# Output projection, squared-ReLU MLP and final norm of an encoder layer: operands prescaled by the input row's norm, a pre-split first chunk, a last chunk by token halves

## The chip, the cores and the metric

One core of one Trainium2 chip runs the whole layer as one program. The metric is the time of one execution in microseconds (us), as the device measures it. Times below come from the runs of the kernel before and from one execution of it that the hardware profiler recorded.

## What is computed

The layer has three mixers on 1152 tokens (1024 of a prompt, 128 of running streams), a merge, an output projection, a channel mixer with a squared ReLU, and a final RMSNorm. D is 1024, the hidden width 4096, everything is float32. The change lies behind the mixers, save for one store and the order of two loads:

```python
def rms_norm(x, g):
    y = x * lax.rsqrt(jnp.mean(x * x, axis=-1, keepdims=True) + EPS)
    return y * g

m = sigmoid(g_a) * y_a + sigmoid(g_b) * y_b + sigmoid(g_c) * y_c
x = x + m @ w_o
u = rms_norm(x, g2) @ w_up
x = x + jnp.square(jax.nn.relu(u)) @ w_down
...
y = rms_norm(x, final_g)
```

## The kernel before

Activations lie transposed: channels on the 128 partitions, tokens along the free dimension, so that a token's norm is a sum over partitions and over 8 column tiles. Float32 accuracy is made from three products: each operand is split into a high part `h` (a cast on ScalarE to the rounded type fp32r) and a low part `l` (a subtraction, mostly on VectorE), and `mm3` multiplies h by h, h by l and l by h into one PSUM sum. Each matmul has 288 columns here (`HP`), two of them make a token half of 576 (`PC`).

Engines run their own instruction streams in order; the code's order is the order on each engine, and semaphores hold an instruction until its inputs are there. So the place of a line in the code decides what stands ahead of it on VectorE (DVE, `V`), ScalarE (ACT, `A`), GpSimd (POOL, `GP`) and on SyncE's DMA queue (SP, `SY`).

**Ahead of the change.** The y units (three mixers' output matrices) end with `y_finish`, which splits the merged m into `mh` and `ml` (L277, L278).

**Output projection (wo).** `back_half` runs 16 units: two token halves by 8 column tiles, 48 matmuls each (L230 to L232). `wo_load` fetches the weights, `wo_split` splits them (L1379, L1359). `Norm.take` adds the unit to the residual x on DVE (L1553), stores x to DRAM (`xs_d`, L1554), squares it on ACT (L1556), and POOL sums the squares.

**Second norm.** `Norm.stat` sums over partitions with small matmuls (L1565), takes the power -1/2 on POOL (L1568), makes a diagonal (L1570); `spread` broadcasts it by two matmuls and an ACT copy (L1581). Only then can `Norm.build` multiply x by norm and gain (L1587), form the Strassen combinations of a pair of column tiles (kk, kk+4) and split them into the operands `H` (ACT L1595, DVE L1359); `build3` splits the last ones. The first token half is built under the units of the second, the second half under the first up run.

**Up.** 16 steps, each a Winograd-Strassen 2 by 2 block: seven products (1, 2, 6, 5, 7, 4, 3) of 24 matmuls over both token halves; the first run is done once per token half (`ra`, `rc`). `SLOTS` fixes what happens between the products: a run issues its own 2, 6, 5, 7, then product 1 of the next run, then 4, 3. Products 1, 6, 7 and 4 add up in one PSUM tile Y, out of which ACT copies between them. `URun.after` makes the four blocks c11, c12, c22, c21, applies max(c,0)*c (`sq`, L1510; c21 on ACT, L1530 and L1531), forms s1 to s4 and stores seven operands (`put`, L1507) to `ad_d`.

**Down.** The 16 hidden steps are taken in `CHUNKS` of 3, 3, 3, 3, 2, 2; for each chunk four runs `d{chunk}{j}`, each seven products again, of 18 matmuls with three steps in the chunk and 12 with two. `feed` loads the operands back (`ar`, L1737) and splits them (ACT L1723, DVE L1359), at most two a slot. `Step.prep` splits the weights (ACT L1420, DVE L1359, four subtractions on POOL). `DRun.after` adds each product to `xt` (DVE, L1362), which `x_back` has loaded (L1710). PSUM has four tiles (`PD`), the pool `E` 16 tiles of 576 columns, the pool `T` 28 tiles of 1152.

**Tail.** After the last run `tail` squares x (ACT, sums on POOL and DVE, L1782, L1362), small matmuls sum over partitions (`fst`, L1815), then `fr` (L1817, L1818), `fdg` (L1821), `frb` (L1826), `frs` (L1828), and the last multiplications (DVE L1835, POOL L1832 and L1833) with the stores (L1837). It handles 576 columns at a time, hf 0 and then hf 1.

## Time and profile before

| | us |
|---|---|
| median of three runs (lowest, highest) | 2121.35 (2120.41, 2127.46) |
| the profiled execution | 2124.79 |
| its span, first to last instruction | 2123.0 |

| engine | busy us | share of the span |
|---|---|---|
| PE (matmul) | 2000.4 | 94% |
| DVE | 1423.1 | 67% |
| ACT | 806.9 | 38% |
| POOL | 798.8 | 38% |

The mean granted clock of TensorE is 0.977 of full speed. Stages, in time from the span's start: in-projection and mixers to 1038, y units to 1189, output projection to 1305, second norm and first up run to 1366, the other up runs to about 1690, six down chunks to 2088, tail to 2123. A PE that is busy is not a PE at its peak rate: what a stage loses is its length less the number of its matmuls times the time of one in an undisturbed stretch.

### The profile page before, as it was taken

The numbers are of one execution on the slowest core, as the hardware profiler recorded it, in microseconds if no ns is written. First come the engines' busy times: TensorE is split into PE (matmuls) and PEld (weight loads), VectorE is DVE, ScalarE is ACT, GpSimd is POOL, SyncE is SP. The second block draws the span as 40 slices with busy tenths as digits, with TensorE's granted clock in tenths as the row PEclk, the third lists the DMA queues.
The fourth block names the chain that finished last, engine by engine and source line by source line (L and its number), as shares of the span: only waits on it lengthen the run. The fifth ranks groups of instructions, "written<-read, shape, count | busy, mean of one in ns | idle before, by whom it ended". The sixth has DMA issues, their size and how long they took to land.

```text
span 2123.0 us, 37198 instructions
## 1 busy us (share of the span) xinstructions
PE 2000.4 (94%) x14321; PEld 1942.3 (91%) x14321; DVE 1423.1 (67%) x2243; ACT 806.9 (38%) x1501; POOL 798.8 (38%) x714
## 2 busy tenths in 40 slices
PE   8999999999999999999999997799999979999994
PEld 7999999999889999898999997699999979999893
DVE  6688888888755564756346456855565668767775
ACT  5434344343326454453212223332333434323431
POOL 4334533433622452626025224344444332222235
PEclk9999999999999999999999998899999989999997
DMA  5354553435544334332555252244343664424412
GB/s 177 121 144 136 128 148 102 113 106 135 171 139 146 132 100 138 119 122 82 201 193 177 89 167 88 82 145 151 132 148 134 215 231 146 157 93 138 132 56 89
DMA packets 202832, 287.66 MB, mean 135 GB/s; under 512 B 47032, under 2 KB 135928, under 8 KB 202656
## 3 DMA queue, kind: packets, MB, share of 16 engines
q1 hardware_dynamic: 202656, 285.29, 42.0%
q8 instruction: 113, 1.85, 0.4%
q14 instruction: 63, 0.52, 0.1%
HBM read 189.14 MB, written 96.08 MB: 134 GB/s over the span
## 4 chain that ended last, share of the span: by engine, by line
PE 51%; DVE 7%; POOL 5%; issue 4%; ACT 2%; DMA 2%; SPq 0%; DVEq 0%; POOLq 0%; ACTq 0%
PE u L230 6%; PE u L232 6%; PE u L231 5%; PE d L230 4%; PE d L232 4%; PE d L231 4%; PE pc L230 3%; PE pc L232 3%; PE pc L231 3%; PE y L232 2%; PE y L230 2%; PE y L231 2%; POOL g L1073 2%; POOL g L1074 1%; DVE a L1359 1%
## 5 line engine op out<-in xcount | busy, mean ns | idle before, releaser
L230 PE MATMUL pc<-hh,wh 128*128 128x384 f32 x1248 | 441.2, 354 | 7.5 <-ACT wh L201 5.2
L232 PE MATMUL pc<-hh,wl 128*128 128x384 f32 x1248 | 424.8, 340 | 2.0 <-DVE wl L213 2.0
L231 PE MATMUL pc<-hl,wh 128*128 128x384 f32 x1248 | 424.3, 340 | 1.1 <-DVE hl L377 1.0
L230 PEld LDWEIGHTS pc<-hh,wh 128*128 128x128 f32 x1248 | 237.0, 190 | 17.0 <-ACT wh L201 5.2
L231 PEld LDWEIGHTS pc<-hl,wh 128*128 128x128 f32 x1248 | 237.1, 190 | 4.6 <-DVE hl L377 3.1
L232 PEld LDWEIGHTS pc<-hh,wl 128*128 128x128 f32 x1248 | 236.4, 189 | 2.5 <-DVE wl L213 2.3
L1362 DVE TENSOR_TENSOR xt<-xt,d 128x576 f32<-128x576 f32 x168 | 126.1, 750 | 91.5 <-PE d L232 91.2
L539 DVE SCALAR_TENSOR_TENSOR y<-up,pv,y 128x768 f32<-128x768 f32 x120 | 132.1, 1101 | 0.2
L213 DVE TENSOR_TENSOR wl<-wr,wh 128x1024 fp32r<-128x1024 f32 (+1 forms) x71 | 92.5, 1305 | 55.6 <-ACT wh L212 55.5
L726 ACT ACTIVATE p<-s,m 128x128 f32<-128x128 f32 (+3 forms) x64 | 47.6, 744 | 178.2 <-DVE m L724 174.0
L542 POOL TENSOR_TENSOR y<-y,ud 128x256 f32<-128x256 f32 x120 | 107.8, 898 | 9.4
L1359 DVE TENSOR_TENSOR a<-ar,a 128x576 fp32r<-128x576 f32 x112 | 94.4, 878 | 13.5 <-ACT a L1723 13.3
L311 POOL TENSOR_TENSOR gt<-gt,gt 128x384 f32<-128x384 f32 x45 | 55.0, 1221 | 125.1 <-DVE gt L310 116.5
L541 POOL TENSOR_TENSOR ud<-up,pv 128x256 f32<-128x256 f32 x120 | 97.7, 814 | 7.4
L232 PE MATMUL y<-bh,wl 128*128 128x384 f32 x288 | 97.5, 339 | 0.0
L231 PE MATMUL y<-bl,wh 128*128 128x384 f32 x288 | 97.0, 337 | 0.0
L230 PE MATMUL y<-bh,wh 128*128 128x384 f32 x288 | 97.0, 337 | 0.0
L1723 ACT CAST a<-ar 128x576 fp32r<-128x576 f32 x112 | 72.5, 672 | 61.8 <-DMA ar<-ad_d 54.8
L230 PE MATMUL pt<-wh,hh 128*128 128x260 f32 (+1 forms) x288 | 84.9, 295 | 5.4 <-ACT vs L603 4.2
L212 ACT CAST wh<-wr 128x1024 fp32r<-128x1024 f32 (+1 forms) x71 | 74.1, 1046 | 38.2 <-PE y L231 29.0
L231 PE MATMUL pt<-wl,hh 128*128 128x260 f32 (+1 forms) x288 | 81.9, 284 | 0.9 <-DVE wl L213 0.9
L232 PE MATMUL pt<-wh,hl 128*128 128x260 f32 (+1 forms) x288 | 81.8, 284 | 0.0
(829 smaller groups left out, 6179.6 us busy)
## 6 DMA issues: line engine op xcount, KB each, us to landing
wr<-in_wu SPq DMA_DIRECT2D x67, 512.0 KB
ar<-ad_d SPq DMA_DIRECT2D x112, 288.0 KB
gt<-sg SPq DMA_DIRECT2D x24, 576.0 KB
wor<-in_wo SPq DMA_DIRECT2D x32, 256.0 KB
sg<-zgg_a SPq DMA_DIRECT2D x24, 192.0 KB
sg<-zgg_b SPq DMA_DIRECT2D x24, 192.0 KB
...
```

What stands on the lines that cost most here:

```text
L212: A.copy(h[:, :c], r[:, :c])
L213: V.tensor_tensor(out=l[:, :c], in0=r[:, :c], in1=h[:, :c].bitcast(F32), op=ALU.subtract)
L230: PE.matmul(out, lh, rh, start=start, stop=False, skip_group_check=again)
L231: PE.matmul(out, lh, rl, start=False, stop=False, skip_group_check=again)
L232: PE.matmul(out, ll, rh, start=False, stop=stop, skip_group_check=again)
L311: (V if n == 23 else GP).tensor_tensor(out=macc[ct][:, r], in0=macc[ct][:, r], in1=gt[:, r], op=ALU.add)
L539: V.scalar_tensor_tensor(out=y[:, :CD], in0=u[:, j:j + CD], scalar=w, in1=y[:, :CD], op0=ALU.mult, op1=ALU.add)
L541: GP.tensor_tensor(out=tm, in0=u[:, CD + j:NPR + j], in1=wp1, op=ALU.mult)
L542: GP.tensor_tensor(out=yp, in0=yp, in1=tm, op=ALU.add)
L1359: eng.tensor_tensor(out=out, in0=a, in1=b, op=ALU.subtract)
L1362: eng.tensor_tensor(out=out, in0=a, in1=b, op=ALU.add)
L1723: A.copy(t[:, 0:PC], r)
```

## The change

- **Norm factors.** The broadcast factors of the first norm (`rbs`), known since the start, are stored to DRAM (`rs_d`) and loaded as `s0` and `s1`. The up operands are built from x times gain times min(s, 1), and no longer wait for the second norm. The true norm comes in behind the up product, as a factor f in `sq`: DVE takes max(c,0)*f, ACT squares it. The matmuls in `fin` (24 instead of 12) and three small DVE instructions work out f.
- **Order in wo.** Column tiles go 0, 4, 1, 5, ... so that a pair is complete after two units; `build` and the splits stand inside the units from u = 2. Of the second half, build(3) and 16 splits are left for `ra`. m is held as `mm[pc][ct]`, h and l of one token half in a tile, so `y_finish` has pieces cut at token 576; `wo_load` and `wo_split(0)` stand one y unit earlier.
- **Up order.** Step 15 comes first, step 14 last.
- **First chunk split in up.** For steps 0 to 2, `put` splits the operand at once (ACT, DVE) and stores h and l to `ah_d`; chunk 0 loads 21 tiles of 1152 columns and splits nothing. `x_back(1..3)` go into d00, d01 and d02.
- **Down.** Chunks 3, 3, 2, 3, 3, 2. Every third operand split of `feed`, and the weight splits of products 5 and 7, are on POOL.
- **Last chunk.** Four runs by token halves: columns j = 0, 1 and 2, 3 of the first half, then 2, 3 and 0, 1 of the second, each matmul still 288 columns; the weights of two j stand in one step and are kept. `final(0)` normalises and stores the first token half under the last two runs; `final(1)` does the rest behind them, from PSUM, with three of eight columns on ACT and POOL.

The diff, cut to what the text speaks of, with twelve columns of indentation left out:

```diff
-CHUNKS = (3, 3, 3, 3, 2, 2)
+CHUNKS = (3, 3, 2, 3, 3, 2)
+CTS = (0, 4, 1, 5, 2, 6, 3, 7)
...
+        SY.dma_start(rs_d[:, r], rbs[g])
...
-        sub(V, l, self.raw(p), raw(h))
+        sub(GP if p in self.gp else V, l, self.raw(p), raw(h))
...
     def put(self, p, n):
-        SY.dma_start(v2(ad_d[p, self.s])[:, self.pcs[0]:self.pcs[-1] + 1, :], self.buf(n))
-
-    def sq(self, c):
-        V.scalar_tensor_tensor(out=c, in0=c, scalar=0.0, in1=c, op0=ALU.max, op1=ALU.mult)
+        b, c = self.buf(n), slice(self.pcs[0] * HP, (self.pcs[-1] + 1) * HP)
+        if self.s < CHUNKS[0]:
+            h, l = E(f"{self.name}h{p}"), E(f"{self.name}l{p}")
+            A.copy(v2(h).bitcast(F32R), b)
+            V.tensor_tensor(out=v2(l).bitcast(F32R), in0=b, in1=v2(h), op=ALU.subtract)
+            SY.dma_start(ah_d[p, self.s][:, 0:PC], h)
+            SY.dma_start(ah_d[p, self.s][:, PC:2 * PC], l)
+        else:
+            SY.dma_start(v2(ad_d[p, self.s])[:, self.pcs[0]:self.pcs[-1] + 1, :], b)
+
+    def sq(self, c, n, src=None):
+        f = v2(fs[n // 2])[:, self.pcs[0]:self.pcs[-1] + 1, :]
+        V.scalar_tensor_tensor(out=c, in0=c if src is None else src, scalar=0.0, in1=f, op0=ALU.max, op1=ALU.mult)
+        A.activation(c, c, AF.Square)
...
+            self.sq(b(c21), c21, self.ov(self.Y))
...
+        if not fs:
+            fs.extend([E("f0"), E("f1")])
         pt = PD(f"st{self.pc}")
...
+        for j, t in enumerate((self.ss, self.s)):
+            for i in range(6):
+                PE.matmul(pt[0:96, 6 * j + i:6 * j + i + 1], t[:, i * 96:(i + 1) * 96], on1[:, 0:1], start=True, stop=True)
+        self.ss = self.s = None
+        r, w = s8(f"r{self.pc}")[0:96, 0:6], s8(f"w{self.pc}")[0:96, 0:6]
+        V.tensor_scalar(w, pt[0:96, 6:12], 8.0 / D, None, ALU.mult)
+        V.tensor_tensor(out=w, in0=w, in1=w, op=ALU.mult)
+        V.scalar_tensor_tensor(out=r, in0=pt[0:96, 0:6], scalar=EPS, in1=w, op0=ALU.add, op1=ALU.mult)
...
+        for h in range(2):
+            A.copy(fs[h][:, self.pc * HP:(self.pc + 1) * HP], pv2(o)[:, h, :])
...
+            V.tensor_scalar(self.s, self.s, 1.0, None, ALU.min)
...
+            V.scalar_tensor_tensor(out=t, in0=t, scalar=par("g2", k), in1=self.s, op0=ALU.mult, op1=ALU.mult)
...
+            self.e[kk // 2] = E(f"se{self.pc}{kk}")
+        self.split(1, kk)
+        self.split(2, kk)
+        e = self.e[kk // 2][:, kk % 2 * HP:(kk % 2 + 1) * HP]
+        add(GP, e, a[:, t2], b[:, t2])
+        sub(GP, a[:, t2], a[:, t1], a[:, t2])
+        sub(GP, a[:, t1], e, a[:, t1])
+        sub(GP, b[:, t1], b[:, t1], a[:, t1])
...
+    if u >= 2:
+        q, r = divmod(u - 2, 8)
+        N, kk = norms[q], r // 2
+        if r % 2 == 0:
+            N.build(kk)
+            if q == 0:
+                N.split(4, kk)
+        else:
+            for p in (6, 5, 7) if q == 0 else (6,):
+                N.split(p, kk)
...
-            next(blds, None)
+        for kk in range(4):
+            N0.split(3, kk)
+        N0.x.clear()
+        N0.fin()
+    if u == 10:
+        N0.spread()
...
+rest = [(p, kk) for p in (5, 7, 4, 3) for kk in range(4)]
...
 def hook_a(slot):
     if slot == 0:
-        N1.stat()
+        N1.split(6, 3)
     elif slot == 2:
+        N1.fin()
+    elif slot == 4:
         N1.spread()
-    elif slot > 2:
-        for _ in range(3):
-            next(bl1, None)
-
+    for _ in range(3):
+        if rest:
+            N1.split(*rest.pop(0))
+
+N1.build(3)
...
-        sub(V, t[:, PC:2 * PC], r, raw(t[:, 0:PC]))
+        sub(GP if nf[0] % 3 == 2 else V, t[:, PC:2 * PC], r, raw(t[:, 0:PC]))
+        nf[0] += 1
...
+        if c == 0:
+            t = acts[key] = T("a{}{}{}".format(*key), F32R)
+            SY.dma_start(t.bitcast(F32), ah_d[p, k])
+            continue
...
+                add(V, x, x, pv2(o)[:, i, :])
+                if p in FIN:
+                    done.append((self.pc, ch, hf))
...
+sA = Step("dA", dsrc(c, 0, True), CHUNKS[c], True)
+sB = Step("dB", dsrc(c, 2, True), CHUNKS[c], True, wide=True)
+for j, step, pc in ((0, sA, 0), (2, sB, 0), (2, sB, 1), (0, sA, 1)):
+    r = DRun(c, j, step, pc)
+    r.end, r.keep = (pc, j) == (1, 0), True
+    runs.append(r)
...
+def square(pc, ch, hf, eng=GP):
+    if ss[pc] is None:
+        ss[pc] = T(f"ss{pc}")[:, 0:PC]
+    t = ss[pc][:, hf * HP:(hf + 1) * HP]
+    seen[pc] += 1
+    if ch == (0, 2)[pc] + 4 * hf:
+        A.activation(t, xv(pc, ch, hf), AF.Square)
+        return
+    q = T(f"fq{pc}{ch}{hf}")[:, 0:HP]
+    A.activation(q, xv(pc, ch, hf), AF.Square)
+    add(eng, t, t, q)
+
...
+def final(pc):
+    last = seen[pc] < 16
+    if last:
+        for x in sorted(done, key=lambda x: -x[2]):
+            square(*x, V)
+        done.clear()
+    assert seen[pc] == 16
+    o = PD(f"fst{pc}")
+    dg = T(f"fdg{pc}")[0:96, 0:PC]
+    rr = s8(f"fr{pc}")[0:96, 0:6]
+    rb = None if last else T(f"frb{pc}")[:, 0:PC]
+    hs = ((1,), (0,)) if last else ((0, 1),)
+    for h in hs:
+        c = slice(3 * h[0], 3 * h[-1] + 3)
+        for i in range(c.start, c.stop):
+            PE.matmul(o[0:96, i:i + 1], ss[pc][:, i * 96:(i + 1) * 96], on1[:, 0:1], start=True, stop=True)
+        r = rr[:, c]
+        V.tensor_scalar(r, o[0:96, c], EPS, 1.0 / D / D, ALU.add, ALU.mult)
+        diag(dg[:, h[0] * HP:(h[-1] + 1) * HP], r, 3 * len(h))
+    del o
+    yield
+    ob = PD(f"fsb{pc}")
+    for h in hs:
+        for hf in h:
+            PE.matmul(pv2(ob)[:, hf, :], on1[0:96, :], dg[:, hf * HP:(hf + 1) * HP], start=True, stop=True)
+    yield
...
+    if not last:
+        A.copy(v2(rb), pv2(ob))
+        del ob
+    for hf in (1, 0):
+        r = pv2(ob)[:, hf, :] if last else rb[:, hf * HP:(hf + 1) * HP]
+        if last and hf == 1:
+            rb = T(f"frb{pc}")[:, 0:PC]
+            for h in (1, 0):
+                A.copy(rb[:, h * HP:(h + 1) * HP], pv2(ob)[:, h, :])
+        for ch in (1, 0, 2, 4, 3, 5, 6, 7):
+            x = xv(pc, ch, hf)
+            if ch in (1, 4, 6):
+                A.mul(x, x, par("fg", ch))
+                GP.tensor_tensor(out=x, in0=x, in1=rb[:, hf * HP:(hf + 1) * HP], op=ALU.mult)
             else:
-                add(V if j == 3 else GP, ss[hf], ss[hf], q)
-
+                V.scalar_tensor_tensor(out=x, in0=x, scalar=par("fg", ch), in1=r, op0=ALU.mult, op1=ALU.mult)
+            SY.dma_start(O["y"][ch * P:(ch + 1) * P, pc * PC + hf * HP:pc * PC + (hf + 1) * HP], x)
+            n += 1
+            if n % 2 == 0:
+                yield
...
+                x_back(0)
+        if n is last_u and slot == 4:
             TF[0] += 4
+        if isinstance(r, DRun) and r.c == 0 and r.j < 3 and slot == 1:
+            x_back(r.j + 1)
...
+        if isinstance(r, DRun) and r.pc is not None:
+            for f in fins:
+                next(f, None)
+            while done and not (r is runs[-1] and slot > 5):
+                square(*done.pop(0))
+            if seen[0] == 16 and not fins:
+                fins.append(final(0))
...
             wo_load(0)
             wo_load(1)
+        if (br, j) == (2, 3):
+            wo_split(0)
```

The code moves instructions on every engine. **DVE, from the last output unit into the first up run.** `x217` is column tile 7 of the second token half; `H302` is product 3's operand of the first half, `u00e0` (`u150e0`) the first block c11 of the first up run. Before:

```order
L1553 SCALAR_TENSOR_TENSOR x217_13449<-wo15_13533,x217_13449 128x576
L1362 TENSOR_TENSOR sq10_13036<-sq10_13036,sq17_13605 128x576
L1359 TENSOR_TENSOR U0l6_13609<-U0r6_13599,U0h6_13608 128x512
...
L1359 TENSOR_TENSOR H300_13628<-x204_12619,H300_13628 128x288
...
L1359 TENSOR_TENSOR H302_13633<-x206_12755,H302_13633 128x288
...
L1567 TENSOR_SCALAR r1_13673<-st1_13666 96x6
L1570 TENSOR_TENSOR dg1_13676<-cst_77,r1_13673 96x576
L1362 TENSOR_TENSOR u00e0_13651<-u00e0_13651,u00_2_13653 128x288
L1510 SCALAR_TENSOR_TENSOR u00e0_13651<-u00e0_13651 128x288
L1587 SCALAR_TENSOR_TENSOR x210_12891<-x210_12891,pv_79,rb1_13710 128x576
L1587 SCALAR_TENSOR_TENSOR x214_13197<-x214_13197,pv_79,rb1_13710 128x576
```

After:

```order
L1593 SCALAR_TENSOR_TENSOR x217_13545<-wo15_13630,x217_13545 128x576
L1369 TENSOR_TENSOR U15l6_13703<-U15r6_13693,U15h6_13702 128x512
...
L1643 SCALAR_TENSOR_TENSOR x213_13475<-x213_13475,pv_79,s1_12974 128x576
L1643 SCALAR_TENSOR_TENSOR x217_13545<-x217_13545,pv_79,s1_12974 128x576
L1369 TENSOR_TENSOR H112_13607<-x213_13475,H112_13607 128x288
L1369 TENSOR_TENSOR H212_13610<-x217_13545,H212_13610 128x288
L1369 TENSOR_TENSOR H612_13679<-x213_13475,H612_13679 128x288
L1369 TENSOR_TENSOR H510_13762<-se10_13305,H510_13762 128x288 x2
L1369 TENSOR_TENSOR H512_13767<-se12_13606,H512_13767 128x288
L1372 TENSOR_TENSOR u150e0_13745<-u150e0_13745,u150_2_13747 128x288
L1538 SCALAR_TENSOR_TENSOR u150e0_13745<-u150e0_13745,f0_13211 128x288
```

The norm's steps (L1567, L1570) and the first product with its factor (L1587 by `rb1`) stood ahead of every operand of the second half; now the operands of pair 3 are multiplied by `s1` at once, and the operands of pairs 0 to 2 already stand in the wo units.

**ACT, in an early up run**, from the last weight split ahead of the c12 copy to the c21 block. `u10e1` (`u00e1`) is c12, copied out of Y behind product 6; `u10e0` is c11, `u10e3` c22. Before:

```order
L1420 CAST U2h1_14078<-U2r1_13992 128x512
L1523 COPY u10e1_14112<-u10_1_13963 128x576
L1420 CAST U2h2_14139<-U2r2_13994 128x512
L1420 CAST U2h6_14171<-U2r6_14143 128x512
L1525 COPY u10e3_14175<-u10_1_13963 128x576
L1420 CAST U2h5_14205<-U2r5_14109 128x512
```

After:

```order
L1435 CAST U1h1_14135<-U1r1_14048 128x512
L1539 ACTIVATE u00e0_14052<-u00e0_14052 128x576
L1529 CAST u00h1_14142<-u00e0_14052 128x576
L1552 COPY u00e1_14175<-u00_1_14019 128x576
L1435 CAST U1h2_14202<-U1r2_14050 128x512
L1435 CAST U1h6_14234<-U1r6_14206 128x512
L1554 COPY u00e3_14238<-u00_1_14019 128x576
L1539 ACTIVATE u00e3_14238<-u00e3_14238 128x576
L1529 CAST u00h4_14243<-u00e3_14238 128x576
L1435 CAST U1h5_14274<-U1r5_14172 128x512
```

Two instructions that need c11 from DVE (its square and the cast for `ah_d`) now stand ahead of the copy of c12, and two more behind that of c22.

**SP's queue at the boundary of up and down**, as it stands ahead of and among the loads of `x_back(0)`. Before:

```order
L1737 DMA ar109_17503<-ad_d_103 128x576 x2
L1737 DMA ar107_17506<-ad_d_103 128x576 x2
L1507 DMA ad_d_103<-u150e0_17388 128x576
L1737 DMA ar105_17576<-ad_d_103 128x576 x2
L1710 DMA xt00_17611<-xs_d_102 128x576
L1710 DMA xt40_17613<-xs_d_102 128x576
L1710 DMA xt41_17615<-xs_d_102 128x576
L1710 DMA xt01_17617<-xs_d_102 128x576
L1737 DMA ar103_17625<-ad_d_103 128x576 x2
```

After:

```order
L1784 DMA a012_17702<-ah_d_104 128x1152
L1784 DMA a020_17704<-ah_d_104 128x1152
L1784 DMA a021_17706<-ah_d_104 128x1152
...
L1534 DMA ad_d_105<-u140e0_17592 128x576
L1784 DMA a060_17742<-ah_d_104 128x1152
L1784 DMA a061_17744<-ah_d_104 128x1152
L1784 DMA a062_17746<-ah_d_104 128x1152
...
L1758 DMA xt00_17820<-xs_d_103 128x576
L1758 DMA xt40_17822<-xs_d_103 128x576
L1758 DMA xt41_17824<-xs_d_103 128x576
L1758 DMA xt01_17826<-xs_d_103 128x576
L1784 DMA a072_17828<-ah_d_104 128x1152
```

Loads of 128x1152 (h and l) stand where loads of 128x576 stood, ahead of the last up run's first store.

## Rows read from the trace of the kernel before

**Rows 1.** Windows by stage, last an undisturbed 50 us: busy us (instructions) by engine, clock.

```profile
core 0: us, PE busy (x) PEld busy (x) DVE busy (x) ACT busy (x) POOL busy (x), PEclk, DMA share, GB/s
1038.00:1189.40 151.40, 151.33 (x864) 151.01 (x862) 78.55 (x131) 33.85 (x61) 55.11 (x46) 1.00 0.46 161
1189.40:1304.60 115.20, 109.54 (x784) 108.06 (x784) 61.09 (x83) 35.52 (x71) 30.81 (x28) 0.96 0.46 148
1304.60:1365.60 61.00, 38.31 (x212) 35.17 (x211) 52.22 (x90) 25.69 (x63) 18.48 (x14) 0.75 0.17 54
1365.60:1689.10 323.50, 323.50 (x2449) 323.50 (x2448) 186.50 (x221) 103.21 (x176) 143.57 (x90) 1.00 0.43 145
1697.90:1780.10 82.20, 71.14 (x507) 70.74 (x506) 59.71 (x88) 33.17 (x62) 22.41 (x18) 0.92 0.58 205
1780.10:1988.50 208.40, 201.17 (x1508) 199.43 (x1507) 154.85 (x233) 79.24 (x149) 54.28 (x48) 1.00 0.42 135
1988.50:2039.90 51.40, 46.50 (x339) 46.06 (x338) 40.14 (x69) 15.82 (x37) 14.16 (x16) 0.97 0.29 89
2039.90:2088.20 48.30, 43.75 (x324) 42.84 (x323) 29.89 (x48) 15.41 (x34) 23.10 (x22) 1.00 0.08 25
2088.20:2123.00 34.80, 6.84 (x32) 4.54 (x32) 20.16 (x20) 3.11 (x5) 18.18 (x9) 0.57 0.40 136
1450.00:1500.00 50.00, 50.00 (x380) 50.00 (x379) 28.94 (x34) 16.66 (x28) 21.72 (x13) 1.00 0.42 141
```

**Rows 2.** What PE waited for from 1150 us on: total us, times, longest.

```profile
PE d L230 <- DVE xt L1362: 25.0, 13, 7.4
PE frb L1826 <- DVE fdg L1821: 12.8, 2, 9.3
PE u L230 <- ACT H L1595: 10.5, 3, 5.1
```

**Rows 3.** DVE's groups by shape, 1304.6 to 1365.6: busy us, mean ns, idle before.

```profile
L1359 DVE TENSOR_TENSOR H<-x,H 128x288 fp32r<-128x288 f32 x35 | 18.7, 586 | 2.9 <-ACT H L1595 2.5
L1587 DVE SCALAR_TENSOR_TENSOR x<-x,pv,rb 128x576 f32<-128x576 f32 x8 | 7.2, 946 | 2.4 <-ACT rb L1581 2.4
```

**Rows 4.** Timeline of POOL at the end of wo: start, duration, instruction.

```profile
1303.55 1.68 POOL L1359 TENSOR_TENSOR x<-x,x 128x288 f32<-128x288 f32 x2
1318.80 1.33 POOL L1568 TENSOR_TENSOR r<-r,cst 96x6 f32<-96x6 f32 x1 [5.75 <-DVE r L1567]
```

**Rows 5.** Windows of 10 us at the boundary of up and down.

```profile
1690.00:1700.00 10.00, 10.00 (x78) 10.00 (x77) 9.08 (x15) 7.38 (x15) 1.00 (x1) 1.00 1.04 388
1700.00:1710.00 10.00, 5.11 (x39) 4.88 (x37) 9.83 (x11) 3.55 (x7) 4.32 (x4) 0.88 1.04 402
```

**Rows 6.** Timelines of DVE, then ACT, in an undisturbed up run.

```profile
1478.86 0.76 DVE L1510 SCALAR_TENSOR_TENSOR u50e<-u50e 128x576 f32<-128x576 f32 x1
...
1483.02 0.64 ACT L1523 COPY u60e<-u 128x576 f32<-128x576 f32 x1 [5.86 <-PE u L232]
...
1496.40 0.69 ACT L1531 ACTIVATE u60e<-u60e 128x576 f32<-128x576 f32 x1
```

**Rows 7.** Tiles a, xt and H on DVE, whole span: duration ns least/median/most.

```profile
L1359 DVE TENSOR_TENSOR a<-ar,a x112: 743/751/1956, 1677.4 to 2028.5; 128x576 fp32r<-128x576 f32 x112
...
L1362 DVE TENSOR_TENSOR xt<-xt,d x168: 740/754/755, 1695.0 to 2088.2; 128x576 f32<-128x576 f32 x168
...
L1359 DVE TENSOR_TENSOR H<-x,H x56: 440/452/1679, 1264.2 to 1353.6; 128x288 fp32r<-128x288 f32 x56
```

**Rows 8.** Timelines of DVE and POOL in the tail.

```profile
2088.88 3.15 DVE L1362 TENSOR_TENSOR fq<-fq,fq 128x576 f32<-128x576 f32 x4
...
2099.78 7.72 DVE L1835 SCALAR_TENSOR_TENSOR xt<-xt,pv,frs 128x576 f32<-128x576 f32 x6 [3.17 <-ACT frs L1828]
...
2111.28 7.23 DVE L1835 SCALAR_TENSOR_TENSOR xt<-xt,pv,frs 128x576 f32<-128x576 f32 x6 [3.11 <-ACT frs L1828]
...
2093.54 2.28 POOL L1818 TENSOR_TENSOR fr<-fr,cst 96x12 f32<-96x12 f32 x1 [10.09 <-DVE fr L1817]
...
2104.14 1.53 POOL L1833 TENSOR_TENSOR xt<-xt,frs 128x576 f32<-128x576 f32 x1
```

More of the change, by code (lines that the diff above doesn't have):

```diff
@@ L276, in y_finish @@
                 ct, r = yfin.pop(0)
-                A.copy(mh[ct][:, r], macc[ct][:, r])
-                V.tensor_tensor(out=ml[ct][:, r], in0=macc[ct][:, r], in1=mh[ct][:, r].bitcast(F32), op=ALU.subtract)
+                for pc in range(2):
+                    a, b = max(r.start, pc * PC), min(r.stop, pc * PC + PC)
+                    if a < b:
+                        t = mm[pc][ct]
+                        h, l = t[:, a - pc * PC:b - pc * PC], t[:, a - pc * PC + PC:b - pc * PC + PC]
+                        A.copy(h, macc[ct][:, a:b])
+                        V.tensor_tensor(out=l, in0=macc[ct][:, a:b], in1=h.bitcast(F32), op=ALU.subtract)
                 if r.stop == NTOK:
@@ L1693, in back_half @@
             go(ra, None, hook_a)
-            for _ in bl1:
-                pass
-            for kk in range(4):
-                N1.build3(kk)
+            assert not rest
+            N1.x.clear()
+            N1.e.clear()
             rc.mm(1)
@@ L1710, in x_back @@
                     SY.dma_start(t, xs_d[ch, hf])
-            K0 = [sum(CHUNKS[:c]) for c in range(len(CHUNKS))]
-            for c in range(len(CHUNKS)):
+            K0 = [sum(CHUNKS[:c]) for c in range(NC)]
+            for c in range(NC):
                 for p in (1, 2, 6, 5, 7, 4, 3):
@@ new lines, in back_half @@
+            runs = [rc] + [URun(s, (0, 1), ustep(s)) for s in UO[1:]]
+            last_u = runs[-1]
+            for c in range(NC - 1):
+                for j in range(4):
+                    r = DRun(c, j, Step(f"d{c}{j}", dsrc(c, j), CHUNKS[c], gp=(5, 7)))
+                    r.end = j == 3
+                    runs.append(r)
+            c = NC - 1
+            sA = Step("dA", dsrc(c, 0, True), CHUNKS[c], True)
[3 more added lines that the diff above has]
+                r.end, r.keep = (pc, j) == (1, 0), True
+                runs.append(r)
@@ L1799, in hook @@
                     feed()
-                    if n is not None:
+                    if n is not None and n.step is not r.step:
                         n.step.prep(slot)
-                    if nn is not None:
+                    if nn is not None and nn.step is not n.step and nn.step.at == 0:
                         nn.step.load(slot)
-                    if slot == 0 and isinstance(r, DRun) and r.c == len(CHUNKS) - 1 and r.j:
-                        tail(r.j - 1)
-                go(r, n, hook)
@@ L1808, in back_half @@
-                if isinstance(r, URun) and r.s == NST - 1:
-                    x_back(2)
-                    x_back(3)
-            tail(3)
-            pt = PD("fst")
-            for hf in range(2):
-                for i in range(6):
-                    PE.matmul(pt[0:96, hf * 6 + i:hf * 6 + i + 1], ss[hf][:, i * 96:(i + 1) * 96], on1[:, 0:1], start=True, stop=True)
-            r = T("fr")[0:96, 0:12]
-            V.tensor_scalar(r, pt[0:96, 0:12], 1.0 / D, EPS, ALU.mult, ALU.add)
-            GP.tensor_tensor(out=r, in0=r, in1=mhalf[0:96].to_broadcast([96, 12]), op=ALU.pow)
@@ L1839, in trunk @@
+            for _ in final(1):
+                pass
         with pool("ps2", PSUM) as ps:
```

270 lines of the change are left out of this document (123 added, 147 removed).

## The prediction, made before the change was run

> **What bounds the kernel now.** I read the windows by stage first [rows 1]: PE is the engine that sets the pace, but only where it is fed. The undisturbed stretch of the up runs does 380 matmuls in 50 us, 7.6 per us or 131.6 ns each, at full granted clock. Against that rate each stage shows what it loses: the length less the matmuls divided by 7.6 (for whole chunks I use the nominal 504 or 336 matmuls, 66.3 or 44.2 us, since a few records are missing). Output projection: 115.2 - 784/7.6 = 12.0 us. Second norm with the first up run: 61.0 - 212/7.6 = 33.1. The other up runs: nothing (2449 matmuls in 323.5 us). Chunk 0: 82.2 - 66.3 = 15.9. Chunks 1 to 3: 208.4 - 198.9 = 9.5. Chunk 4: 7.2. Chunk 5: 4.1. Tail: 34.8, all of it. The sum is some 117 us, and no change that keeps the matmuls can win more; this one keeps them. Then the waits of PE [rows 2]: 25.0 us on DVE's additions to xt in down, 10.5 on the operands H in the first up run, 12.8 on the diagonal in the tail. These are DVE's queues, not DVE's work: PE waits for what stands last in a row. In the norm stage DVE is busy 52.2 of 61 us, so there DVE is the bound.
>
> **Output projection.** wo_split(0) and its loads move ahead of the last y unit; they cost PE nothing there, since PE is busy 151.33 of 151.40 us and DVE only 78.55, and the 16 more small pieces of y_finish (about 0.45 us of DVE each pair) lie in the same cover; without it they would be 4 us. The start of wo no longer waits for the split, but the units get more DVE work (two more products by gain and some 16 more splits, 61 + 12 = 73 of 115 us) and 24 instead of 12 small matmuls (1.1 us). I keep 4 of the 12 us: +8, between +5 and +12.
>
> **Second norm and first up run.** What DVE has left from the end of wo until rc can run: one addition of x (0.75), five weight splits (0.68 each by the 751 ns for 576 columns, 3.4), two products by gain (0.8 each, between 0.75 and the 946 ns of [rows 3], 1.6), 17 splits of H at 0.45 [rows 7], 7.7, the small ones of the norm 1.3, 18 half-width instructions of the two half runs at 0.45, 8.1, and seven weight splits, 4.8. Together 27.6 us. The power on POOL is now under the product, but DVE stands still for it once, 1.3, and once for POOL's four additions of pair 3, 2.5 of the 4 x 0.84 us [rows 4]. Where POOL works beside it, a split of H took 586 ns in the mean instead of 452 [rows 3, 7]; a quarter on top is 7.4. So about 39 us against 61: +22. The floor is PE's 28 to 30 us (+31); if the slowest DVE instructions of before come back, it is 48 (+13).
>
> **Up runs with pre-split stores.** Each of steps 0 to 2 gets seven DVE subtractions (0.75 by [rows 7]) and seven ACT casts (0.64 by [rows 6]), and every run four squares on ACT (0.69) for one relu and one square. A run is 168 matmuls, 22.1 us; DVE is busy 186.5/323.5 of that now, 12.7 us, and ACT 7.0 [rows 1]. They come to some 18 and 13: no engine is full. But the order counts. The order shows two ACT instructions on c11 ahead of the copy of c12, and these wait for DVE's product on c11, which stands behind the run before's s1, s2 and two low parts, one of which waits for POOL. Behind the waiting copy is PE: product 7 adds to the same PSUM tile Y and may start only when c12 is out. It is due 3 products after the run starts, 3 x 3.16 = 9.5 us. Counted through the queues, with POOL's subtraction at 1.5 to 2 us, the copy comes some 4 us late in each of three runs, with the first of them pushed by rc's rest, and the same chain is felt once more in step 3: 16 us. Nothing of before shows this wait; the nearest bounds are an undisturbed run, in which the copy takes 0.64 us as soon as PE is done [rows 6], with some 5 us for the first run, and twice the delay when all DVE instructions go at their slow values: -16, between -5 and -27. From step 3 on the run has only the c21 product (0.76) more on DVE and two squares more on ACT, with DVE at 13.5 of 22.1 us: nothing.
>
> **Boundary of up and down.** Chunk 0 no longer splits 21 operands (21 x (0.75 + 0.67)), which fell where DVE is busy 9.08 and 9.83 of 10 us and PE at 39 of 76 matmuls [rows 5]. In exchange 21 loads of 576 KB instead of 288: 12.4 MB, with 1.2 MB of xt, about 2 of stores and 2 of weights some 17.6 MB. The two windows show 388 and 402 GB/s at a full queue, so 44 us, against some 36 us of time for it: the last up run's 22.1 less a slot of 3 (its tiles come free product by product) and d00's 16.6. SP issues in order: loads that wait for tiles hold the last up run's stores and the four xt loads, and DVE waits for these with d01's splits queued behind. x_back(1..3), 12 loads of 288 KB, move into d00 to d02, 3.5 MB that this peak is rid of. I keep 10 of 15.9 us: +6, between -4 and +12. The Trainium skill ("DMA: Bandwidth & Descriptors", Bandwidth) puts the limit of HBM for a core at some 358 GB/s; by that the 17.6 MB would take 49 us and the term would be +1. The two windows are above it, and I go by them.
>
> **Chunks 1 to 5.** The matmuls are the same. A third of the later splits goes to POOL (about 30 x 1.53 [rows 8], and 40 weight splits): DVE gets 0.75 x 30 + some 0.6 x 40 = 46 us back in 380, with no loss where it was not full. A chunk of two steps now stands ahead of one of three: 12 products' slots of 1.6 us have to feed 21 operands at two a slot, and chunk 4 of before shows what short slots lose, 7.2 us. I give each boundary of equal chunks 2 us (two of them), the two-step chunk 1.3, its two edges 7 and 6, and the last chunk 2.8: 21.5 against 20.8, so -1. If the edges cost nothing more than the others it is +7, if they cost double and half of the POOL time falls on DVE -10.
>
> **Tail.** 34.8 us are a chain over 576 columns twice [rows 8]: squares and four additions 3.2, sums, power 2.3, diagonal, spread, copy, six products 7.7, again a spread and copy, six products 7.2, and 4.5 us from the last product (2118.5) to the end. Half of it moves under the last two runs. What stays, at 288 columns: additions and squares 2, sums and small ones 0.8, power 0.9 (1.33 for six columns in [rows 4], 2.28 for twelve), diagonal and spread 1.0, hand-overs between engines 1.5 to 3, ten products of 0.5, and 4.5 for the last store: 15.7 to 17.2; I take 17.5 with a copy. +17, between +13 and +20.
>
> **Sum.** 8 + 22 - 16 + 6 - 1 + 17 = 36 us of the profiled execution's 2124.79, so 2088.8. That execution is 3.4 us above the median; from the median 2121.35 it is **2085 us**.
>
> **Rivals.** (a) *Everything fits*: c12 is never late (0 for -16), the loads of chunk 0 land in time (+12), the edges give 3 back, wo and norm come out two us better each: 10 + 24 + 0 + 12 + 3 + 17 = 66, 2055 us. For it: DVE has a third of its time free in the up runs. Against: the in-order queues.
> (b) *POOL's splits block DVE.* The row shows a split of a, both inputs in SBUF, at 743 to 1956 ns, and an addition out of PSUM never over 755 [rows 7]. So an instruction with two SBUF inputs is stretched beside POOL. POOL gets 30 x 1.53 + 40 x 1.0 (two thirds of 1.53 for 384 columns) = 86 us more in down; DVE is at two-input work some 40% of the time, which is 34 us of delay, of which half is hidden: 17 us, 2102. The Trainium skill ("SBUF — State Buffer", Who interferes with whom) has it as a lock: a DVE instruction with two inputs in SBUF and a GpSimd instruction that reads SBUF hold each other off for the whole of one. By this rule it would be so; the trace agrees in that 1956 ns is about 751 plus one POOL instruction. That DVE had idle time in each slot speaks against half of it being felt.
> (c) *The first chunk's pre-split loses*: 27 in the runs of step 0 to 2, -4 at the boundary, edges -10: 36 - 11 - 10 - 9 = 6, 2115.
> (d) *Slower.* The new ACT squares and the c21 product out of PSUM are in all 15 full up runs, not in three. If the chain to the c12 copy is later than 9.5 us in each, PE waits in each. Break-even is 52 us (the sum without the -16) by 15, 3.5 us a run; at 5 us it is 75, and 2121 + 23 = 2144. For it: one ACT instruction more stands ahead of c12. Against: DVE has 9 and ACT 15 us idle in a run of 22.1.
> (e) *The norm stays in the way*: the 16 splits left for ra and the POOL additions make DVE as late as before, +5 for +22: 2102.
>
> **How the numbers follow.** Forecast 0.46, (a) 0.20, (b) 0.12, (c) 0.10, (d) 0.07, (e) 0.05. A measurement of this kernel can tell some 0.3% (6.4 us) from no change; (c) lies on that bound, so that half of it is no change: faster 0.46 + 0.20 + 0.12 + 0.05 + 0.03 = 0.86, same 0.07, slower 0.07. The forecast's own bounds, taken together, are 20 us either way. The range goes from 2052, (a) with a little more, to 2112, short of (c): left out are (d), most of (c) and some of (a), under 0.2.
>
> **What would show it.** The windows by stage: wo about 107 us, the norm stage 39, up runs 0 to 2 at 26 to 27 us each for 22.1, chunk 0 at 76, the end of the last matmul to the end of the span 17.5. In the waits of PE, u L230 on the copy of c12 tells (c) and (d) from (a), with its count: three runs or all. In the rows of tile a on DVE, a median above 0.9 us in down tells (b). I am wrong if the queues' delays in steps 0 to 2 are hidden, or if chunk 0's loads arrive late enough to stall all of d00.

## The result, and the profile after

The changed kernel took 2139.38 us in the median of four runs (2138.34 to 2141.64), the kernel before 2123.76 beside it, also in four: the ratio is 1.0075, 95% interval 1.0053 to 1.0097. It is slower by 0.75% or 16 us, clear of noise, where 36 us of gain were forecast. The profiled execution took 2138.73 us; its span is 2136.9 against 2123.0.

The stages of the changed kernel, in windows as in [rows 1] (busy us and instructions by engine, granted clock, DMA share, GB/s): output projection, norm stage with the first up run, the next four up runs, the eleven after them, chunk 0, chunks 1 to 4, chunk 5, tail.

```profile
core 0: us, PE busy (x) PEld busy (x) DVE busy (x) ACT busy (x) POOL busy (x), PEclk, DMA share, GB/s
1189.70:1296.30 106.60, 106.60 (x799) 106.32 (x799) 78.60 (x109) 41.77 (x87) 47.15 (x43) 0.98 0.50 166
1296.30:1343.20 46.90, 32.53 (x221) 31.30 (x221) 26.06 (x49) 18.10 (x45) 18.19 (x16) 0.89 0.18 57
1343.20:1459.60 116.40, 97.69 (x674) 96.75 (x673) 76.25 (x91) 47.78 (x81) 40.21 (x25) 0.91 0.46 162
1459.60:1703.10 243.50, 243.50 (x1844) 243.50 (x1843) 158.09 (x171) 87.30 (x151) 105.81 (x68) 1.00 0.47 163
1703.10:1793.60 90.50, 71.91 (x508) 71.02 (x506) 50.36 (x65) 26.41 (x50) 38.26 (x32) 0.91 0.69 248
1793.60:2063.40 269.80, 251.86 (x1845) 250.07 (x1844) 192.86 (x247) 96.60 (x185) 139.88 (x118) 0.97 0.39 122
2063.40:2116.90 53.50, 47.36 (x340) 46.18 (x339) 34.82 (x73) 19.93 (x45) 32.37 (x35) 0.97 0.16 51
2116.90:2136.90 20.00, 4.63 (x16) 2.80 (x16) 7.95 (x20) 4.12 (x10) 6.25 (x8) 0.55 0.34 118
```

Set beside [rows 1], stage by stage:

| stage | before | after | gain | forecast (bounds) |
|---|---|---|---|---|
| output projection | 115.2 | 106.6 | +8.6 | +8 (5 to 12) |
| norm stage, first up run | 61.0 | 46.9 | +14.1 | +22 (13 to 31) |
| next four up runs | 4 x 22.2 | 116.4 | -27.6 | -16 (-5 to -27) |
| chunk 0 | 82.2 | 90.5 | -8.3 | +6 (-4 to 12) |
| chunks 1 to 5 | 308.1 | 323.3 | -15.2 | -1 (-10 to 7) |
| tail | 34.8 | 20.0 | +14.8 | +17 (13 to 20) |

The sum is -13.6, the spans differ by 13.9. PE's longest waits show where the losses lie (from 1030 us on: what waited, on whom, total us, times, longest; the first six lines of the list):

```profile
PE d00None L233 <- ACT a L1772: 11.5, 1, 11.5
PE u L233 <- ACT u150e L1545: 7.7, 1, 7.7
PE d00None L233 <- DVE xt L1372: 6.0, 2, 5.1
PE u L233 <- ACT u20e L1552: 6.0, 1, 6.0
PE u L233 <- ACT u10e L1552: 5.9, 1, 5.9
PE u L233 <- ACT u30e L1552: 5.2, 1, 5.2
```

L1552 is the copy of c12: the full runs of steps 1, 2 and 3 wait for it, 5 to 6 us each, that of step 0 waits 1.6, and the list has no such wait in the later runs. So the run of step 0 takes 23.9 us and the three behind it 92.5, for 22.2 each before. Two waits in d00, 11.5 and 5.1 us, are the boundary. In the norm stage DVE is busy 26.06 us, near the 27.6 that were counted, but the stage takes 46.9.

**The chain to c12**, timelines of DVE, POOL and ACT in the run of step 1 (start, duration, instruction, idle time before it and its releaser):

```profile
1374.12 3.21 DVE L1530 TENSOR_TENSOR u00l<-u00e,u00h 128x576 fp32r<-128x576 f32 x2 [1.46 <-ACT u00h L1529]
1377.26 1.74 DVE L1369 TENSOR_TENSOR U2l<-U2r,U2h 128x512 fp32r<-128x512 f32 x1
1379.70 1.04 DVE L1538 SCALAR_TENSOR_TENSOR u10e<-u10e,f 128x576 f32<-128x576 f32 x1
...
1374.90 6.96 POOL L1369 TENSOR_TENSOR U2r<-U2r,U2r 128x512 f32<-128x512 f32 x4
...
1380.77 0.68 ACT L1539 ACTIVATE u10e<-u10e 128x576 f32<-128x576 f32 x1 [4.59 <-DVE u10e L1538]
1381.49 0.67 ACT L1529 CAST u10h<-u10e 128x576 fp32r<-128x576 f32 x1
1382.06 0.63 ACT L1552 COPY u10e<-u 128x576 f32<-128x576 f32 x1
```

Read from the bottom: the copy of c12 at 1382.06 stands behind the cast and the square of c11, ACT stood idle 4.59 us for DVE's product on c11, and DVE reached that product late, because two low parts and a weight split ahead of it took 3.21 and 1.74 us (1.5 and 0.68 undisturbed) while POOL formed the four weight sums. The two low parts (`u00l`) are those of the run before, step 0. It fits that the run of step 0 hardly waits: the run before it, step 15, has no pre-split.

### The profile page after: what moved, and what is told of

It is laid out like the page before. It is cut to its first block, busy times and chain, and to the rows that moved or that the text cites. A ratio compares the mean times of both kernels' runs of the same rounds, so it can differ in the third digit from the quotient of the medians.

```text
span 2136.9 us, 37559 instructions
## 1 busy us (share of the span) xinstructions
PE 2008.7 (94%) x14345; PEld 1953.4 (91%) x14345; DVE 1440.7 (67%) x2211; ACT 833.1 (39%) x1560; POOL 902.5 (42%) x814
## 5 line engine op out<-in xcount | busy, mean ns | idle before, releaser
L552 POOL TENSOR_TENSOR y<-y,ud 128x256 f32<-128x256 f32 x120 | 112.7, 939 | 9.4
L1772 ACT CAST a<-ar 128x576 fp32r<-128x576 f32 x91 | 59.0, 671 | 60.5 <-DMA ar<-ad_d 53.7
L1369 DVE TENSOR_TENSOR a<-ar,a 128x576 fp32r<-128x576 f32 x61 | 65.8, 1090 | 18.6 <-ACT a L1772 18.5
L233 PE MATMUL wo<-mm,woh 128*128 128x288 f32 x256 | 76.4, 298 | 0.0
```

What stands on the lines that cost most here:

```text
L233: PE.matmul(out, lh, rh, start=start, stop=False, skip_group_check=again)
L552: GP.tensor_tensor(out=yp, in0=yp, in1=tm, op=ALU.add)
L1369: eng.tensor_tensor(out=out, in0=a, in1=b, op=ALU.subtract)
L1772: A.copy(t[:, 0:PC], r)
```

## The experiments

Times are medians. The ratio beside each is to the kernel before, measured in the same session; where two sessions or chips are compared, go by the ratios. Stages are from the profiled executions, which can be some us faster than the median.

### The three losses, one at a time

**Without the pre-split.** Steps 0 to 2 store plain operands, chunk 0 is loaded and split as the others.

```diff
-                    if self.s < CHUNKS[0]:
+                    if self.s < 0:
...
-                    if c == 0:
+                    if c < 0:
```

> The changed kernel without the pre-split of the first chunk: up steps 0 to 2 store seven plain operands each, chunk 0 loads and splits them as the other chunks do; all else stays. Theory A (the pre-split is what loses: its casts and subtractions delay the copy of c12 in the up runs, its double bytes delay chunk 0): the waits of PE on the copy of c12 after 1343 us vanish (27 us lost there go to about 2), chunk 0 loses 16 us instead of 24, the time falls by 30 to 37 us to about 2104. Theory B (splits on POOL beside DVE are the loss): up runs get better by less than 10, chunk 0 gets no better since its splits now go to POOL by a third, 2125 or more.

2107.55 us, ratio 0.9921 (0.9900 to 0.9942). The four up runs and chunk 0, windows:

```profile
1344.20:1433.00 88.80, 88.80 (x673) 88.80 (x673) 59.41 (x68) 33.32 (x58) 38.81 (x25) 1.00 0.41 139
1677.50:1759.10 81.60, 70.80 (x506) 69.94 (x505) 60.52 (x73) 34.45 (x66) 52.17 (x39) 0.94 0.64 215
```

The up runs are back at 22.2 us each, although the squares on ACT and the c21 product are still in them: rival (d) is out, and without the pre-split c12 is not late. Chunk 0 takes 81.6 us instead of 90.5. Theory A holds: by the stages the pre-split costs 27.6 + 8.9 us (31.8 by the medians), and it gives nothing back, since without it chunk 0 is as long as before the change (82.2).

**Without splits on POOL**, operands and weights of down both on DVE.

```diff
-                    sub(GP if nf[0] % 3 == 2 else V, t[:, PC:2 * PC], r, raw(t[:, 0:PC]))
+                    sub(V, t[:, PC:2 * PC], r, raw(t[:, 0:PC]))
...
-                    r = DRun(c, j, Step(f"d{c}{j}", dsrc(c, j), CHUNKS[c], gp=(5, 7)))
+                    r = DRun(c, j, Step(f"d{c}{j}", dsrc(c, j), CHUNKS[c]))
```

> The changed kernel with all operand splits and weight splits of down on DVE again, none on POOL; all else stays. Theory B (two-input work on DVE is stretched beside POOL, and POOL's own queue delays the weight sums): chunks 1 to 5, which lose 36 us, lose some 22, DVE's mean for a split of a falls from 1090 ns to below 900, the time falls by 10 to 15 us to about 2126. Theory A: DVE is not full in down, the time moves by less than 5 us either way; if DVE is the bound there, it rises by up to 10.

2128.9 us, ratio 1.0018 (1.0007 to 1.0028); chunks 1 to 5 take 315.1 us for 323.3. The splits of operands on DVE by shape, 1740 to 2120 us, first in the changed kernel, where DVE has 57 of them, then here, where it has 86 (busy us, mean ns):

```profile
L1369 DVE TENSOR_TENSOR a<-ar,a 128x576 fp32r<-128x576 f32 x57 | 62.2, 1103 | 6.9 <-ACT a L1772 6.9
```

```profile
L1369 DVE TENSOR_TENSOR a<-ar,a 128x576 fp32r<-128x576 f32 x86 | 70.6, 852 | 6.2 <-ACT a L1772 6.0
```

Moving 29 of 86 splits to POOL saved DVE 8.4 us of busy time instead of 22: those that stayed went from 852 to 1103 ns. Taken one by one, the splits that no POOL instruction overlaps took 748 and 746 ns in the two traces (13 and 59 of them); the overlapped ones 1208 and 1085 (44 and 27). That is rival (b), with its price at 10 us by the medians and 12 by the ratios.

**With the chunks of before.**

```diff
-CHUNKS = (3, 3, 2, 3, 3, 2)
+CHUNKS = (3, 3, 3, 3, 2, 2)
```

> The changed kernel with the chunks 3, 3, 3, 3, 2, 2 of before in place of 3, 3, 2, 3, 3, 2; all else stays. If a two-step chunk ahead of a three-step one is what loses (12.1 us in chunk 2 and its edge to chunk 3), the sum of chunks 1 to 5 falls from 36 to some 28, the time by 5 to 9 us to about 2132. If the edges lose because of POOL whatever the order, the time moves by less than 3.

2135.52 us, ratio 1.0049 (1.0034 to 1.0064), an interval that overlaps that of the changed kernel. Chunks 1 to 5 take 320.8 us, 2.5 less. This is below what was expected of the order; with POOL's splits in place it hardly counts.

### Order or bytes

**The copy of c12 first.** ACT's square of c11 stands behind the copy, in all up runs, and with it the store or pre-split of c11 (the cast on ACT, the low part on DVE). `fac` is the product with f alone, and stays where it was; work and bytes stay.

```diff
                     elif p == 2:
                         add(V, b(c11), b(c11), self.ov(self.X))
-                        self.sq(b(c11), c11)
-                        self.put(1, c11)
+                        self.fac(b(c11), c11)
...
                     elif p == 6:
                         A.copy(b(c12), self.ov(self.Y))
+                        A.activation(b(c11), b(c11), AF.Square)
+                        self.put(1, c11)
```

> The changed kernel with one step of ACT's queue moved: the square of c11, and its store or pre-split, stand behind the copy of c12 and no longer ahead of it, in all up runs. The work, the bytes and the instructions are the same. Theory A' (the place in ACT's queue is the wait): PE no longer waits 6 us for the copy of c12 in three runs, the 27 us lost from 1343 to 1460 fall to 5 to 10, the time by about 18 us to 2121. Rival (DVE's additional work itself is late, so that the next thing behind it becomes the wait): less than 5 us.

2121.05 us, ratio 0.9978 (0.9965 to 0.9992). The four up runs:

```profile
1338.90:1435.70 96.80, 91.47 (x674) 90.54 (x673) 74.18 (x88) 47.08 (x81) 38.62 (x24) 0.98 0.55 193
```

96.8 us for 116.4: with the same work 19.6 of the 27.6 us are gone, so most of the loss was a place in the queue. PE now waits 0.9 to 2.4 us a run for the same copy. (The profiled execution, 2110.09, is the fastest of ten; what the others lose beyond it has no rows. The median moved by 18.3 us, and a second kernel with this order, below, has 96.7 us for the same stretch.)

**The same, with x_back(0) ahead of chunk 0's loads and chunk 1's first splits later.**

```diff
+            def todo_n(c, p):
+                return c == 1 and p == 1
...
-                    fly.append([key, r, 1])
+                    fly.append([key, r, 4 if todo_n(c, p) else 1])
...
-                        if slot == 3:
+                        if slot == 1:
                             x_back(0)
```

> The kernel with the copy of c12 ahead of the square of c11, and two places at the boundary moved: x_back(0) in slot 1 of the last up run instead of slot 3, so ahead of most of chunk 0's loads, and the first three operand splits of chunk 1 three slots later. Bytes and work stay. Theory C (order: DVE stands still behind xt and behind chunk 1's first operand, with d00's additions queued behind): d00 falls from 39 us to 30 or less, the time by 8 to 12 us against the kernel with the copy alone moved (2121). Theory D (bytes: the DMA queue is full for 45 us and d00 can't get its operands earlier): d00 stays above 35, the time moves by less than 4.

2118.32 us, ratio 0.9958 (0.9940 to 0.9976), not clear of the kernel with the copy alone moved; d00 takes 38.5 us for 39.1 there. The trace of the changed kernel had spoken for theory C: DVE idle 13 us for xt at the head of its queue. With xt early the stall is there all the same:

```profile
1683.80:1722.30 38.50, 21.99 (x128) 21.32 (x127) 15.34 (x19) 7.11 (x14) 10.75 (x10) 0.78 0.85 332
```

The chain of work that ended last in this run's trace, 1665 to 1725 us, goes through five loads one behind the other, 39 us of the 60 (start, duration, load):

```profile
1674.80 9.70 DMA a<-ah_d
1684.57 10.32 DMA a<-ah_d
1694.96 9.51 DMA a<-ah_d
1704.48 5.54 DMA ar<-ad_d
1710.08 3.84 DMA ar<-ad_d
```

**The bytes alone.** To the kernel without pre-split, POOL splits and new chunk order (below, 2091.87, 0.9828), 21 copies of 288 KB from DRAM to DRAM that nobody reads.

```diff
                     SY.dma_start(r, ad_d[p, K0[c] + k])
+                    if c == 0:
+                        SY.dma_start(ah_d[p, k], ad_d[p, K0[c] + k])
```

> The same kernel (2091.9) with 21 copies of 288 KB more, one behind each operand load of chunk 0, from DRAM to a DRAM buffer that nobody reads: the bytes of the pre-split alone, with none of its instructions on ACT and DVE. Theory D (bytes): d00, 29.5 us there and 39.0 with the pre-split, takes 36 to 40, the time rises by 7 to 11 us. Theory C (order of the queues): d00 stays below 32.

2099.0 us, ratio 0.9872 (0.9855 to 0.9889), 0.44% more. d00, first without and then with the copies:

```profile
1674.70:1704.20 29.50, 19.68 (x129) 19.01 (x128) 26.70 (x36) 14.44 (x27) 8.94 (x6) 0.83 0.79 273
```

```profile
1679.00:1715.50 36.50, 22.53 (x128) 21.12 (x127) 28.34 (x38) 16.78 (x31) 8.63 (x6) 0.81 0.92 343
```

36.5 us: the copies bring 7.0 of the 9.7 us between 29.5 and the changed kernel's 39.2, and 2.3 more fall on the last up run (24.4 for 22.1). That is what theory D expected. But the copies do not bring bytes alone: each is one more issue on SP's queue, 0.47 us, some 10 us for the 21, and it writes to DRAM as well as reading from it. The pre-split's loads are larger, not more; this run does not part bytes from issues. In the changed kernel the DMA queue is full all through this stretch (windows of 10 us, last columns share and GB/s):

```profile
1690.00:1700.00 10.00, 10.00 (x78) 10.00 (x77) 3.21 (x4) 3.77 (x8) 4.09 (x4) 1.00 1.02 390
1700.00:1710.00 10.00, 5.62 (x43) 5.39 (x41) 0.11 (x1) 0.00 (x0) 0.01 (x1) 0.97 1.02 414
1710.00:1720.00 10.00, 7.53 (x36) 7.29 (x36) 6.29 (x8) 1.77 (x3) 3.39 (x2) 0.69 1.04 420
1720.00:1730.00 10.00, 0.28 (x1) 0.31 (x2) 3.62 (x6) 3.43 (x6) 1.04 (x1) 0.65 1.04 407
```

Before, the queue was full as well from 1690 on, with DVE at 9.08 and 9.83 of 10 us [rows 5]; now DVE does nothing at 1700 and PE nothing at 1720, and both wait for data: DVE for xt, and PE, by the times, for an addition to xt (it ends at 1729.6, PE goes on at 1729.7) that stands in DVE's queue behind the split of a chunk 1 operand, loaded late. With the order moved and nothing gained, the full queue is the cause that is left.

### Together, and what remains

**Without the pre-split, without POOL splits, with the old chunk order** (the three edits above).

> The changed kernel without the pre-split, without splits on POOL, and with the chunks 3, 3, 3, 3, 2, 2: the prescaled operands, the order of the units, the last chunk by token halves and the two-part tail stay. If the three losses found so far are separate, they add up: boundary 82 us as without the pre-split, chunks 1 to 5 together about 312 us instead of 324, some 12 us below the kernel without the pre-split, 2096. If without POOL DVE becomes the bound at the boundary, where all 21 operands of chunk 0 are split again, it gains 6 or less.

2091.87 us, ratio 0.9828 (0.9808 to 0.9848): 1.7% faster than the kernel before, 2.5% than the changed one. Norm stage, four up runs, chunk 0, chunks 1 to 4, chunk 5, tail:

```profile
1293.10:1340.40 47.30, 33.15 (x222) 31.48 (x221) 27.52 (x50) 18.02 (x45) 19.32 (x16) 0.89 0.17 56
1340.40:1430.50 90.10, 89.18 (x675) 88.94 (x674) 60.36 (x70) 34.25 (x60) 38.80 (x25) 1.00 0.42 140
1674.70:1754.20 79.50, 69.68 (x507) 69.01 (x506) 62.35 (x89) 33.25 (x62) 22.25 (x18) 0.94 0.63 212
1754.20:2015.70 261.50, 248.76 (x1844) 247.10 (x1844) 195.04 (x301) 96.05 (x184) 68.01 (x64) 0.99 0.41 128
2015.70:2067.10 51.40, 45.71 (x340) 44.58 (x339) 34.58 (x74) 19.80 (x45) 31.86 (x35) 1.00 0.18 57
2067.10:2086.60 19.50, 4.73 (x17) 2.88 (x16) 7.95 (x20) 4.12 (x10) 6.26 (x8) 0.55 0.35 121
```

The losses add up: by the ratios the three edits gain 1.54, 0.57 and 0.26% alone, 2.37 in sum, and 2.47 together. Chunks 1 to 4 are at 261.5 us against 259.8 before; of the 4.8 us that chunks 1 to 5 still lose to [rows 1], all lie in the last chunk and the run ahead of it (51.4 for 48.3, and 13.1 for 11.2).

**The pre-split kept, with both mends of the order**, no POOL splits, old chunks.

> The pre-split kept, with both mends of the order (copy of c12 first; x_back(0) and chunk 1's first splits moved), no splits on POOL and the chunks 3, 3, 3, 3, 2, 2. It differs from the kernel without all three by the pre-split and the mends alone, so it tells whether the pre-split pays once it stands right: if by theory C its loss is order, it comes within 3 us of that kernel or ahead of it (2090 to 2099); by theory D it stays 10 us or more behind (2106 or more).

2105.95 us, ratio 0.9897 (0.9873 to 0.9922): 14 us behind the kernel without it, 6.6 in the four up runs (96.7 for 90.1), 8.8 at the boundary (88.3 for 79.5). In this order the pre-split still does not pay; that no other order would make it pay is not shown.

**Old last chunk and tail** in the kernel of 2091.87 us: four runs `d5{j}` over both halves and the code of before from `tail` on.

> As the kernel without pre-split, POOL splits and new chunk order, but with the last chunk in four runs over both token halves and the tail behind them, as before the change. It measures the new last chunk by itself: the tail is 34.8 us again for some 20, the last chunk 48 us again for some 52, so 9 to 13 us slower than the kernel with the new last chunk. If the new last chunk disturbs the chunk ahead of it as well (its edge took 20.3 us for 16.7), the difference is only 5 to 8.

2102.25 us, ratio 0.9878 (0.9857 to 0.9899). The last chunk and the tail:

```profile
2016.70:2066.40 49.70, 45.15 (x324) 44.24 (x323) 29.93 (x48) 15.33 (x34) 23.24 (x22) 0.97 0.08 25
2066.40:2101.40 35.00, 7.17 (x32) 4.86 (x32) 20.15 (x20) 3.11 (x5) 18.16 (x9) 0.57 0.39 135
```

The new tail is worth 15.5 us; the new last chunk costs 1.7 of them and the run ahead of it 1.9. The net is 10.4 us by the medians.

**The norm stage.** Pair 3's build ahead of the later weight splits, in the same kernel.

```diff
+            N1.build(3)
             for j in range(3, 7):
                 st0.prep(j)
...
-            N1.build(3)
             ra.mm(1)
```

> The kernel without pre-split, POOL splits and new chunk order (2091.9), with one place moved: the build of pair 3 of the second token half stands ahead of the four later weight splits of the first up run's step, on DVE and ACT, no longer behind them. Theory E (the norm stage is now bound by order: DVE is busy 26 of 46.9 us there, and PE waits 7.7 us for ACT's copy of c11, which stands behind casts of operands that wait for DVE's products by gain, which stand behind five weight splits): that wait falls below 4 us and the time by 4 to 6, to about 2087. Rival (DVE or POOL is the bound of the stage, as the forecast had it): the wait comes back at the next operand, less than 2 us.

2089.25 us, ratio 0.9827 (0.9811 to 0.9843), no difference. PE's wait for the copy of c11 went from 8.5 to 6.6 us, but the first full run ends at 1363.9 us in both. Theory E fell in this form: a chain from the last unit through x, the products by gain, the casts and the copy would be there with one order or the other, but no run tests it, and what remains of the stage (18 us over its matmuls) is not settled.

**POOL's two halves**, each put back alone into the kernel of 2091.87 us (0.9828): the first, then the second pair of lines of the edit that took the splits off POOL is left out.

> The same kernel (2091.9) with every third operand split on POOL again, the weight splits on DVE. If the stretching of DVE's two-input work beside POOL is the loss, the price goes by POOL's time: 30 to 37 splits of 1.45 us, 5 to 8 us slower, and a split of a on DVE goes from 749 ns to 850 or more in the median. If POOL's queue is the loss (weight sums behind splits), the loss shows in the edges of the chunks alone, with waits for weights.

> The same kernel (2091.9) with the weight splits of products 5 and 7 on POOL again, the operand splits on DVE: some 46 splits of 1.0 us. By the stretching theory 3 to 6 us slower; with both together 8 to 11, as found. If only one of the two halves costs, it is not POOL's time as such.

Operand splits: 2109.47 us, ratio 0.9926 (0.9907 to 0.9945). Weight splits: 2100.04 us, 0.9883 (0.9860 to 0.9905). Both cost, 0.98% and 0.55%, more than expected. The prices do not add: the kernel without the pre-split alone has both halves on POOL and the new chunk order besides, and it is 0.93% slower (0.9921 for 0.9828), no more than the operand splits cost by themselves. Why is not shown. DVE's operand splits, 1740 to 2120 us, operand splits on POOL, then weight splits (875 ns without either):

```profile
L1369 DVE TENSOR_TENSOR a<-ar,a 128x576 fp32r<-128x576 f32 x56 | 56.5, 1023 | 5.6 <-ACT a L1772 5.5
```

```profile
L1369 DVE TENSOR_TENSOR a<-ar,a 128x576 fp32r<-128x576 f32 x84 | 76.2, 941 | 0.6 <-ACT a L1772 0.4
```

The stretching is there in both, in the mean; the median split takes 807 and 751 ns, short of the 850 expected for the first, since the splits that no POOL instruction overlaps take 747 and 748 as ever. For the first, the profiled execution (2097.95) is 11 us faster than the median and 9.6 slower than that of the kernel without (2088.39). Its mean granted clock is 0.986, that of the other four 0.978 to 0.982, so its rows don't hold the whole price.

## Why the prediction was wrong, step by step

**Right: the output projection** (+8.6 for +8) **and the tail** (+14.8 for +17). PE waited 5.7 us for the splits of wo's weights before; those waits are gone from the list, as forecast. The tail's additions, spread and products took about the times counted (ten products 4.3 us for 5); short was the last step, 7.0 us from the last product (2129.9) to the end for the 4.5 counted. The last chunk, put at 2.8 us of loss for the 4.1 of before, loses some 5 us more than before with the run ahead of it, in the kernel of 2091.87 us.

**The mechanism of the up runs was right, its size just past the bound** (-27.6 for -16, bound -27). The wait was forecast at the right instruction, product 7 on the copy of c12, behind the low parts of the run before. By that reason it belongs to steps 1 to 3, and there it came; step 0, counted as one of the three, waited 1.6 us. Two things were mis-sized. The copy came 5 to 6 us late and not 4, with the low parts on DVE stretched beside POOL's weight sums (3.21 us for 1.5). And a wait costs more than its length: the run of step 1 lost 8.8 us with 5.9 of waiting. Behind the wait PE's matmuls start 0.24 us apart for 5.7 us and not 0.13, at the lower of its clock's two levels (1.2 and 2.4 GHz); the granted clock in 1367.1 to 1389.0 was 0.84 in the mean, where the undisturbed runs have 1.00.

**The boundary failed in its sign** (-8.3 for +6). The prediction had the bytes (17.6 MB, 44 us against 36 of time) and so 8 us of deficit, and then kept 10 us of stall, fewer than the 15.9 of before, as if the gain of DVE's 21 splits and the deficit of DMA could be set against each other. They can't: before, DVE was late; now the data are late, and d00 can't go on with data that are not there. Chunk 0 loses 24.2 us over its matmuls. DVE's free time bought nothing, as the 8.8 us show by which chunk 0 is longer with the pre-split, mended, than without. This was also the prediction's own sign of being wrong, loads late enough to stall d00. The measured rate at the full queue, 390 to 420 GB/s, was as assumed. It is above the 358 GB/s of the Trainium skill ("DMA: Bandwidth & Descriptors", Bandwidth), as in [rows 5]; that section gives the figure as one core's share when both cores of a pair stream, and only one core works here, so the prediction's second sum for this term (+1) used it where it does not hold.

**Chunks 1 to 5 failed in the credit for POOL** (-15.2 for -1). That DVE gets 46 us back, with no loss where it was not full, was the wrong step, and rival (b), given 0.12 and 17 us, was the right one: taking the splits off POOL brought 8.2 us here and 10 to 12 in all. Its sign, a median split of a above 0.9 us, came just at the bound (0.900). The Trainium skill ("SBUF — State Buffer", Who interferes with whom) says that a DVE instruction with both inputs in SBUF and a GpSimd instruction that reads SBUF hold each other off; the mean of 1103 ns beside 852 agrees. The rest is the new last chunk and the run ahead of it (4.8 us, left in the kernel of 2091.87) and the order of the chunks (2.5 us, for edges put at 13 in a sum that adds to 21.1 us and not 21.5).

**The norm stage gained 14.1 us and not 22.** The work on DVE was counted well (26.06 us busy for 27.6; the quarter on top is 6.9 and not 7.4, which changes little), but the term was made as if DVE would still be the bound. It isn't, with 26.06 busy of 46.9: PE waits there for ACT's copies out of PSUM, the longest 7.7 us. What makes these late is open, since the one order tried changed nothing.

The three largest misses (up runs, boundary, POOL) point the same way, and the rivals took them one at a time. (c) had the first two at -27 and -4, (b) the third at 17; taken together, 36 - 11 - 10 - 17, they give -2, still 12 us above what was measured. No rival joined them. (Of the chance of (c), 0.10, the sum counts 0.03 as faster and 0.07 as no change, not a half each.) Rival (d), the only slower one, came near in time (2144) by the wrong mechanism: the later up runs never waited.
